# Splits of the left operands as single steps over fourteen products, and the first operands and blocks of the down phase loaded apart

## The chip, the cores and the metric

The kernel runs on one core of one Trainium2 chip. Its engines are TensorE (PE; its weight loads are listed apart as PEld), VectorE (DVE), ScalarE (ACT), GpSimd (POOL) and SyncE (SP, which here only issues DMAs). The metric is the device time of one execution in microseconds (us), the median of several runs; less is better. All times of single instructions come from one profiled execution.

## The reference, cut to what matters

One layer of an encoder for 1024 tokens of width 1024: a half-step feed-forward block, a mixer (two groups of attention heads), and a second half-step feed-forward block. The change lies in the two feed-forward blocks alone:

```python
def _swiglu(x, w_gate, w_up, w_down):
    return (jax.nn.silu(x @ w_gate) * (x @ w_up)) @ w_down
...
    f = _swiglu(_rmsnorm(x, ffn1_pre_g[l]), ffn1_w_gate[l], ffn1_w_up[l], ffn1_w_down[l])
    x = x + 0.5 * _rmsnorm(f, ffn1_post_g[l])
...
    f = _swiglu(_rmsnorm(x, ffn2_pre_g[l]), ffn2_w_gate[l], ffn2_w_up[l], ffn2_w_down[l])
    x = x + 0.5 * _rmsnorm(f, ffn2_post_g[l])
```

`w_gate` and `w_up` are 1024 x 2816, `w_down` is 2816 x 1024, all float32.

## The kernel before, in words

**Arithmetic.** Every large product is made of float32r matmuls on operands that are split in two: a high part (ACT rounds the number, `split`, L118) and a low part (the number less the high part, L119, on POOL or DVE). Three passes, high x high, high x low and low x high, make one product (`PASSES`). A feed-forward block is multiplied by a 2x2 block scheme with seven products in place of eight, so sums and differences of blocks are needed on both sides.

**Gate/up phase** (`gate_up`). The 2816 hidden columns are 22 blocks of 128, i = 0 to 21. Block 0 is done plainly. Each block from 1 to 21 is seven products P1, P6, P2, P7, P5, P4, P3, in this order (`ORDER`; the last block has `LAST`), and each product is 12 matmuls of 128x512 (`product`, L294). They share four PSUM banks: P1 and P2 lie in bank a, P6 in b, P7 and P4 in c, P5 and P3 in d (`BANK`), and the second product of a bank adds to what stands there. So three results must be read out before a later product may go on: P1's copy (ACT, L417) before P2; P7's addition (DVE, L422) before P4; P5's addition (DVE, L425) before P3. Each has one other product in between as cover. P2, P5, P4 and P3 end in `glu`: an ACT silu (L452) and a DVE multiplication (L453), which makes the hidden values `h` (DVE's L431 and L434 come ahead of those of P4 and P3). The left operands of later products (weights) are made five ahead (`feed`, `prepare`): ACT makes the high part `wgu`, POOL (for P5 and P3 DVE) the low one, and POOL also makes the differences of the weights (L218, L219 for P6, L228, L230 after P2) that the high parts of the next block wait for.

**Left operands of the down phase** (`keep`). Two blocks, 2j and 2j+1, make pair j (0 to 10). Their four `h` tiles give seven left operands S0 to S6: S0, S1 and S4 are `h` tiles, S5 = S5 + S4, S2 = S5 - S0 (in a new tile of the pool `dn`), S3 = S4 - S2 and S6 = S1 - S2 (L343). Each is split into a row of `y` and stored to DRAM as `hd` (L347), one queue on SP. `keep` puts seven steps into the list `late`, each of them the sum, the high part, the low part and the store of one operand. `run` takes one step off the list ahead of each product, so that in the text the steps of pair j stand at the seven products of the even block 2j+2, and the seven products of the next odd block have none. The steps of the last pair are all done at the end of block 21.

**Order.** The text gives each instruction a place. The order on each engine is fixed when the program is built, and an instruction may be drawn ahead of its place in the text when what it reads is there and its engine has nothing else to do. The tiles of a pool (`dn` has 10 for `h`) are handed out in the order of the text. On the chip each engine then runs its instructions strictly in that fixed order.

**Down phase** (`down`). 77 products of 12 matmuls (L370), k for the operand and j for the pair: first group j = 0 to 4 with k in the order 1, 0, 2, 3, 6, 4, 5, then j = 5 to 10. Each needs two tiles of the left operand from DRAM (`load_left`, L249) and a split right operand made from blocks of `w_down` (`load_block`, L240; `prepare_down`). The first two left operands (`AHEAD`) are loaded into `dn` after the fourth product of block 21, the next three after its last one and behind the steps of the last pair.

Of the kernel before, what the change touches and what calls it, by code (L numbers as in the profile page):

```python
# [10 lines left out]
F32 = mybir.dt.float32  # L11
# [8 lines left out]
S = 1024  # L20
# [16 lines left out]
def tile_macaron_block(ctx, tc, x, f1_pre, f1_post, f1_g, f1_u, f1_d, mix_pre, mix_post, w_qkv,  # L37
# [10 lines left out]
    def f32(ap):  # L48
        return ap.bitcast(F32)
# [71 lines left out]
    class Ffn:  # L121
# [14 lines left out]
        BLOCKS = ("b11", "b12", "b21", "b22")  # L136
        WBUFS = 5
        HBUFS = 10
        AHEAD = 2

        def __init__(self, wg, wu, wd, tag, far):
            self.wg, self.wu, self.wd, self.tag, self.far = wg[0], wu[0], wd[0], tag, far
# [96 lines left out]
            r = self.B[j, name] = self.dw[name].tile([128, 512], F32, name=name)  # L239
            SP.dma_start(r, self.wd[128 * (2 * j + c):128 * (2 * j + c) + 128, 512 * b:512 * b + 512])  # L240

        def load_left(self, n):

            for _ in range(n):
                if self.wanted:
                    key = self.wanted.pop(0)
                    self.A[key] = [self.dn.tile([128, 512], FR, name="h") for _ in range(2)]
                    for z, t in enumerate(self.A[key]):
                        SP.dma_start(f32(t), self.hd[key][:, 512 * z:512 * z + 512])  # L249

        def prepare_down(self, k, j):

            sub, add, tt = OP.subtract, OP.add, DVE.tensor_tensor
            n = len(self.GROUPS[0])
            after = [z for z in ((n,) if j == 0 else ()) + (j + n + 1,) if j < n and z < self.PAIRS]
            if k == 1 and j < n:
                for b in ("b22", "b12", "b11"):
                    self.load_block(j, b)
            b11, b12, b21, b22 = [self.B[j, name] for name in self.BLOCKS]
            self.split_w((j, k), (b11, b21, b11, b12, b12, b11, b22)[k], DVE)  # L260

            def diff(j):
                tt(self.B[j, "b12"], self.B[j, "b22"], self.B[j, "b12"], op=sub)

            if k == 1 and j < n:
                diff(j)
            elif k == 0:
                tt(b11, b12, b11, op=add)
            elif k == 3:
                tt(b12, b21, b11, op=sub)  # L270
            elif k == 4:
                tt(b11, b22, b11, op=sub)
            for z in after:
                for b in {3: ("b21",), 4: ("b12", "b22"), 5: ("b11",)}.get(k, ()):
                    self.load_block(z, b)
                if k == 5:
                    diff(z)
# [56 lines left out]
        def keep(self, j, y):  # L334

            a11, a21, a12, a22 = [self.H[2 * j + c][b] for c in range(2) for b in range(2)]
            S = {0: a11, 1: a12, 4: a22, 5: a21, 3: y[:, 7, 0:512], 6: y[:, 7, 512:1024]}

            def made(n, k, p=None, q=None, op=None):
                if op:  # L340
                    if k == 2:
                        S[k] = self.dn.tile([128, 512], F32, name="h")
                    DVE.tensor_tensor(S[k], S[p], S[q], op=op)  # L343
                st = y[:, n, :]
                hi, lo = [st[:, 512 * z:512 * z + 512].bitcast(FR) for z in range(2)]
                split(hi, lo, S[k], DVE)
                SP.dma_start(self.hd[k, j], st)  # L347

            for n, z in enumerate(((0,), (1,), (4,), (5, 5, 4, OP.add), (2, 5, 0, OP.subtract),
                                   (3, 4, 2, OP.subtract), (6, 1, 2, OP.subtract))):  # L350
                self.late.append(lambda n=n, z=z: made(n, *z))

        def down(self, k, js, y, ps, psd, row=None):
            g = js[0] in self.GROUPS[1]
# [48 lines left out]
        def gate_up(self, i, prod, ps, y, psd):  # L403
# [32 lines left out]
            if i == NF - 1 and n == 3:  # L436
                self.close_tx(3)
                self.raw.release()
                self.load_left(self.AHEAD)
                self.open_blocks(("b11", "b12"), self.far)  # L440
                self.open_blocks(("b22", "b21"), self.near)
                for j in self.GROUPS[0]:
                    self.load_block(j, "b21")
            if n == 6 and i % 2 == 1:
                self.keep(i // 2, y)
            if n == 6 and i == NF - 1:
                self.add_late(7)
                self.load_left(self.HBUFS // 2 - self.AHEAD)
                self.U = [U(name).rearrange("p t f -> p (t f)") for name in ("U2", "U2", "C21", "U3")]

        def glu(self, dst, c, s):
# [3 lines left out]
        def run(self, ps, y, psd, jobs, row):  # L455


            last = self.GROUPS[1][-2:]
            at = self.items.index(("D", 1, self.GROUPS[1][0]))
            for n, it in enumerate(self.items):  # L460
                if n == at:
                    self.add_late(len(self.late))
                    for name in ("b12", "b11"):
                        self.dw[name].release()
                self.feed()
                if not at - 18 <= n < at - 12:
                    self.add_late(1)
                if it[0] == "G":
                    self.gate_up(*it[1:], ps, y, psd)
                    self.used += 1  # L470
                elif it[1:] == (6, last[0]):
                    self.down(6, last, y, ps, psd, row)
                    break
                else:
                    self.down(it[1], it[2:], y, ps, psd)
                    self.used += 1
                    self.load_left(1)
                for job in jobs.get(n - at, ()):
                    job()
            for name in ("b21", "b22"):  # L480
# [726 lines left out]
```

## Time and profile before

| | us |
|---|---|
| median of 3 runs (2145.53 to 2147.35) | 2147.19 |
| profiled execution, own time | 2140.81 |
| its span in the trace | 2139.0 |
| PE busy | 1987.4 |
| DVE busy | 1438.1 |
| ACT busy | 1035.4 |
| POOL busy | 854.3 |

Both feed-forward blocks have the same form: the gate/up phase of the first runs from about 61 us to 524 us of the span, that of the second from about 1431 us to 1902 us, and a down phase follows each. A row of the waits names who waited for whom, and how long in total. A row of the timeline has the start, the length, the engine, the line, the tiles written and read, and in brackets how long the engine had been idle and what ended that. The clock granted to TensorE in the profiled execution was 0.989 of full speed in the mean.

### The profile page before, as it was taken

To read this page: it belongs to the slowest core of one execution; us is meant where nothing else is said; L and a number is where in the kernel's file an instruction comes from. 1 tells how busy PE (TensorE), PEld (TensorE's weight loads), DVE (VectorE), ACT (ScalarE), POOL (GpSimd) and SP (SyncE) were. 2 spreads that over 40 slices of the span, in tenths; PEclk is the share of its full clock that TensorE was granted. 3 is DMA by queue.
4 is the path that set the end of the run, shared out by engine and by line. 5 is a ranking of instruction groups with operands and counts; after the bars stand their busy time and mean duration, and the time that the engine had idled before them with its cause. 6 is when DMAs were issued, how large, how long until landed. Compare 5 with 4: busy or idle time off the path is not lost.

```text
span 2139.0 us, 30720 instructions
## 1 busy us (share of the span) xinstructions
PE 1987.4 (93%) x10704; PEld 1677.0 (78%) x10704; DVE 1438.1 (67%) x2431; ACT 1035.4 (48%) x1977; POOL 854.3 (40%) x768
## 2 busy tenths in 40 slices
PE   7899888998999999999999999999988899879997
PEld 6777667776788899998999998877766777658886
DVE  7765676657555757766998886466567665665566
ACT  5543443434222644546999997344343433433223
POOL 4556555563000002024777886225546555520000
PEclk9999999999899999999999999999999999989999
DMA  4343343435875853232041553213343333468757
GB/s 138 108 138 109 135 141 128 138 109 211 295 261 194 307 160 96 73 104 63 1 134 62 159 141 98 92 48 128 109 147 137 130 128 109 148 245 280 243 194 278
DMA packets 234618, 316.40 MB, mean 148 GB/s; under 512 B 24672, under 2 KB 150624, under 8 KB 234336
## 3 DMA queue, kind: packets, MB, share of 16 engines
q1 hardware_dynamic: 234464, 314.44, 44.0%
q8 instruction: 85, 1.39, 0.3%
q14 instruction: 69, 0.57, 0.1%
HBM read 206.38 MB, written 108.00 MB: 147 GB/s over the span
## 4 chain that ended last, share of the span: by engine, by line
PE 60%; DVE 15%; POOL 9%; ACT 7%; issue 5%; DMA 3%; SPq 0%; DVEq 0%; POOLq 0%; ACTq 0%
PE pd L370 9%; PE pq L612 9%; PE pa L294 6%; PE pt L937 5%; POOL wgu L119 4%; PE pz L1075 4%; PE pd L294 3%; PE pb L294 3%; ACT wgu L118 3%; PE pa L370 3%; PE pb L370 3%; PE po L961 3%; PE pc L370 3%; DVE y L119 3%; DVE y L343 3%
## 5 line engine op out<-in xcount | busy, mean ns | idle before, releaser
L119 POOL TENSOR_TENSOR wgu<-rawgu,wgu 128x512 fp32r<-128x512 f32 x216 | 304.9, 1420 | 449.9 <-ACT wgu L118 435.4
L118 ACT ACTIVATE wgu<-rawgu 128x512 fp32r<-128x512 f32 x302 | 186.4, 625 | 271.9 <-POOL rawgu L230 127.6
L294 PE MATMUL pa<-actT,wgu 128*128 128x512 f32 (+1 forms) x1080 | 269.1, 397 | 48.8 <-ACT U L417 47.9
L294 PEld LDWEIGHTS pa<-actT,wgu 128*128 128x128 f32 x1080 | 199.8, 190 | 103.2 <-ACT U L417 56.8
L370 PE MATMUL pd<-wgu,h 128*128 128x512 f32 x948 | 232.6, 391 | 0.0
L118 ACT ACTIVATE wgu<-b 128x512 fp32r<-128x512 f32 x154 | 96.7, 630 | 276.9 <-PE pd L370 265.4
L612 PE MATMUL pq<-wq,actT 128*128 128x256 f32 x1728 | 214.2, 281 | 0.7 <-DVE vst L623 0.7
L370 PEld LDWEIGHTS pd<-wgu,h 128*128 128x128 f32 x948 | 178.8, 189 | 37.8 <-DVE U L434 0.5
L612 PEld LDWEIGHTS pq<-wq,actT 128*128 128x128 f32 x1728 | 205.9, 188 | 1.0 <-DVE vst L623 0.9
L119 DVE TENSOR_TENSOR wgu<-b,wgu 128x512 fp32r<-128x512 f32 x154 | 105.8, 689 | 147.1 <-ACT wgu L118 146.9
L294 PE MATMUL pc<-actT,wgu 128*128 128x512 f32 x552 | 141.0, 405 | 39.7 <-DVE U L422 39.7
L294 PEld LDWEIGHTS pc<-actT,wgu 128*128 128x128 f32 x552 | 104.3, 192 | 71.9 <-ACT y L118 47.5
L73 POOL TENSOR_SCALAR gpost<-gpost 128x1024 f32<-128x1024 f32 x2 | 2.7, 1330 | 394.8 <-DMA gpost<-in_ffn_post_g_dram 394.8
L840 POOL TENSOR_SCALAR P<-P,il 128x1024 f32<-128x1024 f32 (+1 forms) x128 | 130.1, 1017 | 68.5 <-DVE il L839 62.2
L941 DVE TENSOR_TENSOR PT<-pt,PT 128x512 fp32r<-128x512 f32 (+1 forms) x256 | 146.1, 612 | 2.0 <-ACT PT L940 2.0
L294 PE MATMUL pd<-actT,wgu 128*128 128x512 f32 x552 | 137.4, 397 | 9.4 <-DVE U L425 9.4
L119 DVE TENSOR_TENSOR y<-h,y 128x512 fp32r<-128x512 f32 x110 | 111.2, 1012 | 44.6 <-ACT y L118 44.6
L294 PEld LDWEIGHTS pd<-actT,wgu 128*128 128x128 f32 x552 | 102.1, 188 | 40.3 <-issue 16.7
L940 ACT ACTIVATE PT<-pt 128x512 fp32r<-128x512 f32 (+1 forms) x256 | 125.1, 543 | 12.7 <-PE pt L937 8.6
L937 PE MATMUL pt<-identr,P 128*128 128x128 f32 x896 | 125.4, 275 | 3.1 <-ACT vst L775 2.4
L294 PE MATMUL pb<-tx,wgu 128*128 128x512 f32 x504 | 122.9, 392 | 0.0
L294 PE MATMUL pc<-tx,wgu 128*128 128x512 f32 x504 | 122.5, 392 | 0.0
(205 smaller groups left out, 4024.1 us busy)
## 6 DMA issues: line engine op xcount, KB each, us to landing
hd<-y SPq DMA_DIRECT2D x154, 512.0 KB, 2.7
h<-hd SPq DMA_DIRECT2D x308, 256.0 KB, 3.6
rawgu<-in_ffn_w_gate_dram SPq DMA_DIRECT2D x88, 256.0 KB, 3.1
rawgu<-in_ffn_w_up_dram SPq DMA_DIRECT2D x88, 256.0 KB, 3.5
b<-in_ffn_w_down_dram SPq DMA_DIRECT2D x88, 256.0 KB, 4.5
bkT<-kd SPq DMA_DIRECT2D x32, 320.0 KB, 7.1
rawq<-in_w_qkv_dram SPq DMA_DIRECT2D x16, 512.0 KB, 5.0
bV<-vd SPq DMA_DIRECT2D x8, 640.0 KB, 4.1
```

Source lines behind the costliest of these rows:

```text
L118: ACT.activation(hi, raw, AF.Copy)
L119: return eng.tensor_tensor(lo, raw, f32(hi), op=OP.subtract).ins
L294: PE.matmul(p[:, c0:c1, :], w[:, a, k, :], self.rhs(name, b, k)[:, c0:c1, :], start=(first and n == 0), stop=(n == 11), skip_group_check=True)
L343: DVE.tensor_tensor(S[k], S[p], S[q], op=op)
L370: PE.matmul(p, A[a][:, 128 * i:128 * i + 128], B[:, b, :], start=(first and start and j == js[0] and n == 0), stop=(end and j == js[-1] an ...
L612: PE.matmul(p, actT[:, a, k, T, :], WQ[j][:, b, k, :], start=(n == 0), stop=(n == 23))
L840: POOL.tensor_scalar(P[:, 0:w], P[:, 0:w], il, 1.0, op0=OP.mult, op1=OP.mult)
L937: PE.transpose(out=p[:, j, :], in_=col(P, b0 + j), identity=ident)
L940: ACT.activation(hv, p[:, 0:n, :], AF.Copy)
L941: DVE.tensor_tensor(lv, p[:, 0:n, :], f32(hv), op=OP.subtract)
L961: PE.matmul(o, V[:, k, :], pt[:, a, k, :], start=(n == 0), stop=(n == 15))
L1075: PE.matmul(p[:, 512 * dh:512 * dh + 512], actT[:, a, c, T, :], WO[c][:, b, 512 * dh:512 * dh + 512], start=(n == 0), stop=(n == 23))
```

## The change

`keep` now cuts the same work into fourteen steps, two of them empty. A step holds at most one high part (ACT) and the low part and store of the operand before, or a low part and the next sum. `run` takes one step after each product of the gate/up phase in place of one ahead of it, so in the text the steps of a pair stand over the fourteen products of two blocks. The three sums S2, S3 and S6 and the tile of S2 thereby come later in the text: S2 stands behind P4 of the even block, S3 and S6 at the products of the odd block after it. At the start of the down phase three left operands (not two) are loaded ahead, into a pool `ax` of their own, and five more (not three) behind the last steps; the blocks b11, b22 and b12 of a pair j < 5 are loaded, and their difference is made, when the product k = 0 is prepared and not at k = 1, which needs b21 alone.

```diff
-        AHEAD = 2
+        AHEAD = 3
...
-        def load_left(self, n):
+        def load_left(self, n, pool=None):
...
-                    self.A[key] = [self.dn.tile([128, 512], FR, name="h") for _ in range(2)]
+                    self.A[key] = [(pool or self.dn).tile([128, 512], FR, name="h") for _ in range(2)]
...
-            if k == 1 and j < n:
-                for b in ("b22", "b12", "b11"):
+            if k == 0 and j < n:
+                for b in ("b11", "b22", "b12"):
                     self.load_block(j, b)
-            b11, b12, b21, b22 = [self.B[j, name] for name in self.BLOCKS]
+            b11, b12, b21, b22 = [self.B.get((j, name)) for name in self.BLOCKS]
...
-            if k == 1 and j < n:
-                diff(j)
-            elif k == 0:
+            if k == 0:
+                if j < n:
+                    diff(j)
                 tt(b11, b12, b11, op=add)
...
-            def made(n, k, p=None, q=None, op=None):
-                if op:
-                    if k == 2:
-                        S[k] = self.dn.tile([128, 512], F32, name="h")
-                    DVE.tensor_tensor(S[k], S[p], S[q], op=op)
-                st = y[:, n, :]
-                hi, lo = [st[:, 512 * z:512 * z + 512].bitcast(FR) for z in range(2)]
-                split(hi, lo, S[k], DVE)
-                SP.dma_start(self.hd[k, j], st)
-
-            for n, z in enumerate(((0,), (1,), (4,), (5, 5, 4, OP.add), (2, 5, 0, OP.subtract),
-                                   (3, 4, 2, OP.subtract), (6, 1, 2, OP.subtract))):
-                self.late.append(lambda n=n, z=z: made(n, *z))
+            def half(n, z):
+                return y[:, n, 512 * z:512 * z + 512].bitcast(FR)
+
+            def total(k, p, q, op=OP.subtract):
+                if k == 2:
+                    S[k] = self.dn.tile([128, 512], F32, name="h")
+                DVE.tensor_tensor(S[k], S[p], S[q], op=op)
+
+            def high(n, k):
+                ACT.activation(half(n, HI), S[k], AF.Copy)
+
+            def low(n, k):
+                DVE.tensor_tensor(half(n, LO), S[k], f32(half(n, HI)), op=OP.subtract)
+                SP.dma_start(self.hd[k, j], y[:, n, :])
+
+            steps = [[], [], [(high, 0, 0)], [(low, 0, 0), (high, 1, 1)], [(low, 1, 1), (total, 5, 5, 4, OP.add)],
+                     [(high, 2, 4)], [(low, 2, 4), (total, 2, 5, 0)], [(high, 3, 5)], [(low, 3, 5), (total, 3, 4, 2)],
+                     [(high, 4, 2)], [(low, 4, 2), (total, 6, 1, 2)], [(high, 5, 3)], [(low, 5, 3), (high, 6, 6)],
+                     [(low, 6, 6)]]
+            for step in steps:
+                self.late.append(lambda step=step: [f(*z) for f, *z in step])
...
             if i == NF - 1 and n == 3:
                 self.close_tx(3)
                 self.raw.release()
-                self.load_left(self.AHEAD)
                 self.open_blocks(("b11", "b12"), self.far)
                 self.open_blocks(("b22", "b21"), self.near)
+                self.ax = open_pool("ax" + self.tag, bufs=2 * self.AHEAD, side=self.far)
+                self.load_left(self.AHEAD, self.ax)
...
-                self.add_late(7)
-                self.load_left(self.HBUFS // 2 - self.AHEAD)
+                self.add_late(len(self.late))
+                self.load_left(self.HBUFS // 2)
...
+            at0 = self.items.index(("D", 1, 0))
             for n, it in enumerate(self.items):
                 if n == at:
                     self.add_late(len(self.late))
+                    self.ax.release()
...
-                if not at - 18 <= n < at - 12:
+                if n > at0 and not at - 18 <= n < at - 12:
                     self.add_late(1)
                 if it[0] == "G":
                     self.gate_up(*it[1:], ps, y, psd)
                     self.used += 1
+                    self.add_late(1)
...
-                    self.load_left(1)
+                    if self.used - at0 > self.AHEAD:
+                        self.load_left(1)
```

## Rows read from the trace of the kernel before

**Rows 1.** Waits of PE: who waited for whom, total us, times, longest.

```profile
PE pa L294 <- ACT U L417: 47.9, 22, 2.3
PE pc L294 <- DVE U L422: 39.7, 20, 2.0
...
PE pa L370 <- DMA h<-hd: 19.1, 4, 6.0
```

**Rows 2.** Stretches of blocks 11, 12, 13: length, busy PE, PEld, DVE, ACT, POOL.

```profile
282.11:301.57 19.46, 19.46 (x86) 15.78 (x85) 8.84 (x13) 7.17 (x12) 10.83 (x9) 1.00 0.26 81
301.57:326.58 25.01, 20.17 (x85) 15.53 (x84) 19.96 (x21) 11.05 (x19) 14.24 (x11) 1.00 0.47 169
326.58:346.05 19.47, 19.47 (x86) 15.78 (x85) 8.80 (x13) 7.17 (x12) 10.82 (x9) 1.00 0.26 82
```

**Rows 3.** Timeline of ACT, blocks 11 to 13.

```profile
290.90 0.59 ACT L452 ACTIVATE h<-pa 64x512 f32<-64x512 f32 x1 [2.18 <-PE pa L294]
...
302.63 0.63 ACT L118 ACTIVATE wgu<-rawgu 128x512 fp32r<-128x512 f32 x1 [4.66 <-POOL rawgu L230]
...
308.64 0.63 ACT L118 ACTIVATE y<-h 128x512 fp32r<-128x512 f32 x1 [0.75 <-DVE h L453]
309.18 0.58 ACT L417 ACTIVATE U<-pa 128x512 f32<-128x512 f32 x1
...
312.92 0.59 ACT L452 ACTIVATE h<-pa 64x512 f32<-64x512 f32 x1 [1.60 <-PE pa L294]
...
325.74 0.63 ACT L118 ACTIVATE wgu<-rawgu 128x512 fp32r<-128x512 f32 x1 [1.22 <-POOL rawgu L230]
327.14 0.63 ACT L452 ACTIVATE h<-C 64x512 f32<-64x512 f32 x1 [0.77 <-DVE C L431]
328.52 0.63 ACT L118 ACTIVATE y<-h 128x512 fp32r<-128x512 f32 x1 [0.75 <-DVE h L453]
...
331.23 0.60 ACT L417 ACTIVATE U<-pa 128x512 f32<-128x512 f32 x1
...
335.38 0.59 ACT L452 ACTIVATE h<-pa 64x512 f32<-64x512 f32 x1 [2.18 <-PE pa L294]
```

**Rows 4.** Timeline of DVE, blocks 12 and 13.

```profile
308.64 0.69 DVE L343 TENSOR_TENSOR h<-h 128x512 f32<-128x512 f32 x1
...
310.83 1.37 DVE L119 TENSOR_TENSOR y<-h,y 128x512 fp32r<-128x512 f32 x1 [0.83 <-ACT y L118]
...
313.32 0.68 DVE L343 TENSOR_TENSOR h<-h 128x512 f32<-128x512 f32 x1
...
316.01 1.78 DVE L119 TENSOR_TENSOR y<-h,y 128x512 fp32r<-128x512 f32 x1
317.71 1.76 DVE L343 TENSOR_TENSOR y<-h 128x512 f32<-128x512 f32 x1
319.51 0.69 DVE L422 TENSOR_TENSOR U<-U,pc 128x512 f32<-128x512 f32 x1
...
329.80 0.68 DVE L434 TENSOR_TENSOR U<-U,pd 128x512 f32<-128x512 f32 x1
```

**Rows 5.** Timeline of POOL: one line in block 11 and in block 12.

```profile
294.84 1.29 POOL L219 TENSOR_TENSOR rawgu<-rawgu 128x512 f32<-128x512 f32 x1
...
317.32 1.61 POOL L219 TENSOR_TENSOR rawgu<-rawgu 128x512 f32<-128x512 f32 x1
```

**Rows 6.** Timeline of PE, start of the first down phase.

```profile
523.83 0.86 PE L370 MATMUL pa<-wgu,h 128*128 128x512 f32 x3
...
535.51 1.19 PE L370 MATMUL pa<-wgu,h 128*128 128x512 f32 x2 [6.00 <-DMA h<-hd]
...
542.15 0.80 PE L370 MATMUL pa<-wgu,h 128*128 128x512 f32 x1 [2.89 <-DMA h<-hd]
```

**Rows 7.** Timeline of DVE, end of block 21.

```profile
527.69 1.90 DVE L263 TENSOR_TENSOR b<-b,b 128x512 f32<-128x512 f32 x3
...
532.52 0.69 DVE L343 TENSOR_TENSOR h<-h 128x512 f32<-128x512 f32 x1
```

## What was predicted

> **What bounds the kernel now.** I read the waits of PE first, because PE is the busiest engine and every other engine matters only where PE stands still for it. In the gate/up phases PE waits for two things above all: the ACT copy of P1 (L417), 47.9 us, and the DVE addition of P7 (L422), 39.7 us; at the start of the two down phases it waits 19.1 us for left operands from DRAM [rows 1]. Then the stretches of single blocks, to see where. Odd blocks (11, 13) take 19.46 us, all of it PE: 7 products of 2.78 us. The even block 12, where the text has the operand steps, takes 25.01 us with PE busy for 20.17 [rows 2]. The pattern repeats, so a pair of blocks takes 44.48 us where PE alone needs 38.92. With ten pairs in each of two feed-forward blocks, 5.56 x 20 = 111 us is the most that the gate/up phases could give back.
>
> Third, the timelines of ACT and DVE through such a pair, to see what makes PE wait. I cut the pair at the silu of P2, since a chain starts there. In the **first half**, odd to even, the silu stands at 290.90 and 312.92: 22.02 us. In the **second half**, even to odd, at 312.92 and 335.38: 22.46 us [rows 3]. Both are longer than 19.46. From the silu of P2, ACT makes the high part of the next P1's weights, POOL its low part and differences L218 and L219, ACT and POOL the next two weights, POOL L228 and L230, and only then ACT the next high part: at 302.63 (11.73 us after the silu) and at 325.74 (12.82 us). The silus of P4 and P3 and the copy of P1 are queued on ACT behind that. The copy ends at 309.76 and 331.83, and 3.16 and 3.55 us later comes the next silu of P2 [rows 3]. The first half is thus 11.73 + 7.13 + 3.16, the second 12.82 + 6.09 + 3.55, where about 0.4 of the last term is slack (3.55 less 3.16). So in the first half the chain through ACT and POOL sets the time, and PE waits at P2. In the second half PE is late by itself, because P4 had to wait for L422, which stood on DVE behind operand instructions of 1.78 and 1.76 us [rows 4], and the copy comes just in time.
>
> **What the change moves.** The text spreads the steps, but the order on the engines isn't that of the text. The high part at 328.52 belongs to S0 of the pair 12/13: its place in the text is at P1 of block 14, after 346, and it runs as soon as P4's multiplication has made the tile [rows 3]. S4's high part likewise runs at 308.64, the moment it can, ahead of the copy of P1 at 309.18 that PE waits for [rows 3], though its place is two products behind it; S5's sum follows at 308.64 on DVE [rows 4]. A later place in the text doesn't hold such an instruction back. So S0, S1, S4 and S5 should stay where they are, and with them the first half: I cost it at 22.02, no change.
>
> S2 is the exception. Its inputs are there when S5's sum ends (309.33), and DVE idles for 0.83 us before 310.83, yet S2 runs at 313.32, right after the silu of P2 at 312.92 [rows 3, 4]. That silu is the first to write the `h` tile that is handed out ahead of S2's tile. After the change P5's tile is handed out first as well, and P5's multiplication is the first to write it. S2 then can't come before that, and S2's split, S3 and S6 with their splits hang on it. These are three sums and three low parts on DVE, and three high parts on ACT, which move by two products, from between P2 and P4 to between P5 and the next P1.
>
> What goes: L422 no longer stands behind them, so P4's wait (39.7 us in all) and the smaller one at P3 go. L219 shows 1.29 us with DVE idle and 1.61 with DVE's sums running [rows 5], so POOL's chain gets shorter ahead of P5. What is late next is the copy of P1 of the odd block, since now PE comes sooner and the six DVE instructions stand nearer to it. The second half afterwards:
> - Silu of P2 to the high part behind L230: 11.73 as in the first half, where no operand work runs beside it. DVE's sums now meet up to four POOL instructions (two low parts, L228, L230), 0.32 us each: 11.73 to 13.01. I take two, 12.37.
> - From there to the end of the copy: 6.09 now. It can lose the 0.77 us that ACT waits for L431 and the 1.28 from S0's high part (328.52) to L434 (329.80) [rows 3, 4], if S0 gets behind L434: 4.04. It can gain a sum of 1.76 [rows 4] and a high part of 0.63 with nothing lost: 8.48. I take 4.04 + 0.63 for S3's high part + 0.7 for one sum that meets no POOL instruction, 5.4, because P4's multiplication, which S0 waits for, gets later too.
> - P2 itself to its silu: 3.16 when PE waits for the copy.
>
> The sum is 20.93, against 22.46: 1.53 per pair, 31 us for 20 pairs. Bounds: 11.73 + 4.04 + 3.16 = 18.93 is under PE's 19.46, so at best 3.00 per pair, 60 us; 13.01 + 8.48 + 3.16 = 24.65 costs 2.19 per pair, 44 us. I lean from 31 to 28, since the last pair of each phase has block 21 with its own order.
>
> The stores go with the low parts on SP. I cost them at nothing: of PE's long waits none is for a load of weights [rows 1]. If a late store stood ahead of a weight load, the high part of the next P1 would wait, and that would be part of the 44 us.
>
> **Start of the down phase.** PE begins at 523.83, does two products, waits 6.00 us until 535.51 for the third left operand and 2.89 before 542.15 for its low tile [rows 6]; the second feed-forward block has the other 10.2 us of the 19.1 [rows 1]. Three operands loaded ahead give PE a product of 2.78 us more: 2 x 2.78 = 5.6 us is the least saving. The most is all 19.1. Further, the fourth operand takes `dn` tiles of the pair before the last, so it waits for no tile of the last pair, only for S2's tile to be handed out. S2 at 532.52 stood behind the differences of the blocks, three in 1.90 us at 527.69 and one more [rows 7], which now get a place behind the steps: S2 about 2.5 us sooner. So 2 x (2.78 + 2.5) = 10.6 for certain work, and about half of the low tiles' waits: I take 15. Two more tile loads on SP ahead of the blocks are hidden under the last three products of block 21; without that cover they would lengthen the same wait. The blocks b11, b22 and b12 can be fetched as soon as their pools open, wherever the text has them; were b11 late, ACT's split for k = 0 would hold up only splits behind it, five products ahead of PE.
>
> Sum: 28 + 15 = 43 us. The profiled execution took 2140.8, 6.4 under the median of the runs; taken off the median, 2147.2 - 43 = **2104 us** (the profiled execution would be near 2098).
>
> **Rivals.** Measurements of this kernel tell 0.2%, 4.3 us, from no change.
> - *Both halves at PE's pace.* The steps really spread and no wait is left: 111 + 15 = 126 us, 2021. For it: DVE is busy for 28.8 us and ACT for 18.2 of a pair's 44.5 [rows 2]. Against it: the first half has S4's high part ahead of the copy, and nothing holds it back.
> - *The order stays.* If S2 was held by something else than its tile, DVE's order stays as it is and only the down phase gains: 2147 - 15 = 2132. For it: in the text of before, S2 also stands behind others. Against it: the idle 0.83 us of DVE.
> - *Slower: the copy of the odd block is held up.* The six DVE instructions meet POOL between P5 and the next P1 and stand ahead of P4's multiplication and L434. At the upper bound this costs 44 us and leaves 44 - 15 = 29: 2176. It decides from 0.75 us per pair on (15 / 20): a second half above 23.2 us, which is the copy's end more than 20.0 us after the silu of P2. For it: operand instructions take up to 1.78 us in place of 0.69 where POOL runs beside them [rows 4]. Against it: P5 to P1 leaves DVE about 11 us.
> - The Trainium skill (SBUF — State Buffer, section "Who interferes with whom") has a rule that speaks for this rival: a VectorE instruction with both inputs in SBUF and a GpSimd one that reads SBUF take turns on one port pair, and the loser stands still for the whole of the other. By that an operand instruction could take up to 0.69 + 1.29 = 1.98 us, an estimate; the trace agrees so far as its longest of these rows is 1.78, and L422 and L434, which read PSUM, stay at 0.69.
>
> **How the numbers follow.** Forecast as above, 0.62, by itself from 2068 (60 + 19) to 2138; order stays 0.13; both at PE's pace 0.08; slower 0.12; the two terms cancel within 0.2%, 0.05. Faster is 0.62 + 0.13 + 0.08 = 0.83. The range 2066 to 2148 holds the forecast, the kept order and the cancelling, 0.80, and leaves out the two far cases.
>
> **What would show it.** Right: even blocks lose the wait before P4 (L422's row near nothing), the wait of P2 for L417 stays in even blocks and appears in odd ones, S2 runs right after P5's multiplication, a pair takes about 43 us; the first down wait falls below 2 us. Wrong: L417's wait gone in even blocks (then far faster), S2 still beside the silu of P2 (then only the down phase moves), or a pair above 44.5 us.

## The result, and the profile after

The kernel after takes **2117.24 us** (median of 4 runs, 2112.03 to 2119.59), the kernel before on the same chip 2146.36 (4 runs). The ratio is 0.986, 95% interval 0.984 to 0.988: 29 us or 1.4% faster. The forecast was 2104 with a range of 2066 to 2148. In the profiled executions the span goes from 2139.0 to 2117.1, 21.9 less. PE's busy time rises by 12.2 us to 1999.6, though no matmul is added, and the mean granted clock falls from 0.989 to 0.981.

First the waits of PE after the change (who waited for whom, total us, times, longest). L425 is the copy of P1, L378 a matmul of the down phase, L118 ACT's rounding to a high part.

```profile
PE pa L294 <- ACT U L425: 61.7, 40, 2.6
PE pa L378 <- DMA h<-hd: 14.6, 2, 7.3
...
PE pa L378 <- ACT wgu L118: 5.2, 2, 2.9
```

The row of P7's addition, 39.7 us in [rows 1], is gone. The copy's wait is there 40 times in place of 22: in both blocks of a pair. The wait for left operands has lost 4.5 us, but one for ACT's split has come up.

The windows of block 11, of the even block 12, and then of P2 alone in block 12 and in block 4 (length, busy PE, PEld, DVE, ACT, POOL, granted clock, DMA share, GB/s):

```profile
271.20:291.67 20.47, 19.72 (x86) 15.69 (x85) 13.52 (x18) 8.74 (x15) 12.86 (x11) 1.00 0.45 154
291.67:315.23 23.56, 21.25 (x86) 16.84 (x85) 13.28 (x16) 9.36 (x16) 12.05 (x9) 0.93 0.34 112
...
299.93:304.40 4.47, 4.47 (x13) 3.52 (x14) 2.75 (x4) 1.50 (x3) 1.29 (x1) 0.62 0.87 312
...
127.12:129.80 2.68, 2.68 (x12) 2.19 (x13) 1.85 (x3) 1.51 (x3) 1.31 (x1) 1.00 0.95 331
```

A pair took 19.46 + 25.01 in [rows 2]; it is 20.47 + 23.56 now. The operand work is spread over both: DVE is busy for 13.5 and 13.3 us, where it was 8.8 and 20.0. The third row is P2 of block 12: 4.47 us at a granted clock of 0.62, a mean of stretches at 2.4 and at 1.2 GHz. The last row is the same product in block 4: 2.68 us at 1.00. From block 4 to block 18, even blocks without such a fall take 22.04 us, those with one 23.56.

The timeline of ACT, through block 12 to the silu of P2 in block 13 (L461 silu, L348 an operand's high part):

```profile
281.00 0.59 ACT L461 ACTIVATE h<-pa 64x512 f32<-64x512 f32 x1 [2.12 <-PE pa L294]
...
292.75 0.63 ACT L118 ACTIVATE wgu<-rawgu 128x512 fp32r<-128x512 f32 x1 [4.66 <-POOL rawgu L230]
...
298.76 0.63 ACT L348 ACTIVATE y<-h 128x512 fp32r<-128x512 f32 x1 [0.75 <-DVE h L462]
299.30 0.58 ACT L425 ACTIVATE U<-pa 128x512 f32<-128x512 f32 x1
...
304.58 0.59 ACT L461 ACTIVATE h<-pa 64x512 f32<-64x512 f32 x1 [3.14 <-PE pa L294]
...
317.00 0.63 ACT L118 ACTIVATE wgu<-rawgu 128x512 fp32r<-128x512 f32 x1 [2.23 <-POOL rawgu L230]
...
321.29 0.60 ACT L425 ACTIVATE U<-pa 128x512 f32<-128x512 f32 x1
...
325.05 0.59 ACT L461 ACTIVATE h<-pa 64x512 f32<-64x512 f32 x1 [2.12 <-PE pa L294]
```

S4's high part still runs at the moment it can, just ahead of the copy (298.76, 299.30), as at 308.64 and 309.18 in [rows 3]. The second half, 304.58 to 325.05, is 20.47 us.

The timeline of DVE at the same place (L345 the sums, L351 the low parts, L439 the addition ahead of P4's silu):

```profile
311.70 0.71 DVE L462 TENSOR_TENSOR h<-C,U 64x512 f32<-64x512 f32 x1 [0.96 <-ACT C L461]
312.42 1.69 DVE L345 TENSOR_TENSOR h<-h 128x512 f32<-128x512 f32 x1
314.14 1.67 DVE L345 TENSOR_TENSOR y<-h 128x512 f32<-128x512 f32 x1
315.73 0.68 DVE L439 TENSOR_TENSOR C<-U,pc 128x512 f32<-128x512 f32 x1
...
322.50 1.83 DVE L351 TENSOR_TENSOR y<-y 128x512 fp32r<-128x512 f32 x1
```

S2 now runs right behind P5's multiplication (311.70, 312.42). In [rows 4] it stood at 313.32, after P2.

The start of the first down phase, on PE and on SP's queue:

```profile
511.96 0.56 PE L378 MATMUL pa<-wgu,h 128*128 128x512 f32 x1 [2.27 <-ACT wgu L118]
...
529.93 1.62 PE L378 MATMUL pa<-wgu,h 128*128 128x512 f32 x3 [7.35 <-DMA h<-hd]
```

```profile
492.24 7.45 SPq L352 DMA_DIRECT2D hd<-y  x4
499.77 1.83 SPq L240 DMA_DIRECT2D b<-in_ffn_w_down_dram  x2
501.70 2.85 SPq L249 DMA_DIRECT2D h<-hd  x6
504.82 7.46 SPq L240 DMA_DIRECT2D b<-in_ffn_w_down_dram  x10
...
519.84 5.13 SPq L352 DMA_DIRECT2D hd<-y  x5
525.02 9.81 SPq L249 DMA_DIRECT2D h<-hd  x12
```

Three operands are ahead, so three products run before the long wait and not two; but the wait is 7.35 us where [rows 6] had 6.00 and then 2.89, and one of 2.27 us stands in front of the first matmul (2.95 in the second phase).

### The profile page after: what moved, and what is told of

Read it like the earlier page. It is cut to its first block, busy times and chain, and to the rows that moved or that the text cites. A ratio compares the mean times of both kernels' runs of the same rounds, so it can differ in the third digit from the quotient of the medians.

```text
span 2117.1 us, 30680 instructions
## 1 busy us (share of the span) xinstructions
PE 1999.6 (94%) x10704; PEld 1692.5 (80%) x10704; DVE 1399.4 (66%) x2431; ACT 1032.7 (49%) x1977; POOL 849.5 (40%) x768
## 5 line engine op out<-in xcount | busy, mean ns | idle before, releaser
L119 POOL TENSOR_TENSOR wgu<-rawgu,wgu 128x512 fp32r<-128x512 f32 x216 | 309.4, 1441 | 435.8 <-ACT wgu L118 428.7
L294 PE MATMUL pa<-actT,wgu 128*128 128x512 f32 (+1 forms) x1080 | 289.5, 419 | 61.7 <-ACT U L425 61.7
L118 ACT ACTIVATE wgu<-rawgu 128x512 fp32r<-128x512 f32 x302 | 182.6, 625 | 317.3 <-POOL rawgu L219 155.8
L294 PEld LDWEIGHTS pa<-actT,wgu 128*128 128x128 f32 x1080 | 211.2, 202 | 126.1 <-ACT U L425 78.2
L378 PE MATMUL pd<-wgu,h 128*128 128x512 f32 x948 | 231.1, 390 | 0.0
L118 ACT ACTIVATE wgu<-b 128x512 fp32r<-128x512 f32 x154 | 96.2, 630 | 257.9 <-PE pd L378 227.0
L378 PEld LDWEIGHTS pd<-wgu,h 128*128 128x128 f32 x948 | 177.9, 188 | 37.4 <-DVE U L442 0.5
L294 PE MATMUL pc<-actT,wgu 128*128 128x512 f32 x552 | 136.5, 396 | 0.0
L953 ACT ACTIVATE PT<-pt 128x512 fp32r<-128x512 f32 (+1 forms) x256 | 125.0, 543 | 13.5 <-PE pt L950 11.0
L351 DVE TENSOR_TENSOR y<-h,y 128x512 fp32r<-128x512 f32 x110 | 101.7, 925 | 30.6 <-ACT y L348 30.6
```

What stands on the lines that cost most here:

```text
L118: ACT.activation(hi, raw, AF.Copy)
L119: return eng.tensor_tensor(lo, raw, f32(hi), op=OP.subtract).ins
L294: PE.matmul(p[:, c0:c1, :], w[:, a, k, :], self.rhs(name, b, k)[:, c0:c1, :], start=(first and n == 0), stop=(n == 11), skip_group_check=True)
L351: DVE.tensor_tensor(half(n, LO), S[k], f32(half(n, HI)), op=OP.subtract)
L378: PE.matmul(p, A[a][:, 128 * i:128 * i + 128], B[:, b, :], start=(first and start and j == js[0] and n == 0), stop=(end and j == js[-1] an ...
L953: ACT.activation(hv, p[:, 0:n, :], AF.Copy)
```

## Experiments

Steps are those of `keep`. A "fall" is a product at a granted clock below 1.00 behind a wait of PE. In the expectations, e4 is the experiment with the high parts behind the copy, e9 the one with both edits, e8 the order of the loads, and e10 the sums behind P3's multiplication.

**The steps alone.** The kernel after with the start of the down phase as before:

```diff
-        AHEAD = 3
+        AHEAD = 2
...
-            if k == 0 and j < n:
-                for b in ("b11", "b22", "b12"):
+            if k == 1 and j < n:
+                for b in ("b22", "b12", "b11"):
...
+                self.load_left(self.AHEAD)
...
-                self.ax = open_pool("ax" + self.tag, bufs=2 * self.AHEAD, side=self.far)
-                self.load_left(self.AHEAD, self.ax)
...
-                self.load_left(self.HBUFS // 2)
+                self.load_left(self.HBUFS // 2 - self.AHEAD)
...
```

> The fourteen steps of the change, with the start of the down phase as it was before. Theory: the whole gain of 29 us is made in the gate/up phases, because S2, S3 and S6 move behind P5, and the new start of the down phase trades its waits for others and nets nothing. Then this run is near the changed kernel, 2114 to 2124 us. Rival, the prediction's second term: the down phase gives 15 us, and this run is 2128 to 2136.

Measured 2127.13 us, ratio 0.990 (0.989 to 0.992): between the two. The gate phases lose 20.2 us of their span. But from the end of the last gate product to the start of the sixteenth product of the down phase, the two phases together take 117.8 us where the kernel before takes 110.0, although nothing of the down phase was changed. PE waits 2.06 and 3.27 us in front of the first product, where it had no wait, and 11.36 and 11.38 us for the third operand in place of 6.00 and 5.96. So the spread steps themselves cost 7.8 us there. The timeline of PE, first phase:

```profile
533.97 1.62 PE L378 MATMUL pa<-wgu,h 128*128 128x512 f32 x3 [11.36 <-DMA h<-hd]
```

**The down phase alone.** The kernel before with the new start of the down phase, and `keep` with its seven steps.

> The steps as before, the start of the down phase as in the change. Theory (the down phase nets nothing): 2142 to 2150 us, with a wait for b21 or for the fourth left operand where the third was waited for. Rival (it gives 10 to 19 us): 2128 to 2137.

Measured 2136.64, ratio 0.994 (0.993 to 0.996): 11 us less than the kernel before beside it, as its rival said. PE has no wait in front of the first product, and the first fifteen products take 50.15 and 51.81 us in place of 54.62 and 55.66: 8.3 us less.

**Seven steps, those from S2 on one product later.** The kernel before with one empty step:

```diff
             for n, z in enumerate(((0,), (1,), (4,), (5, 5, 4, OP.add), (2, 5, 0, OP.subtract),
                                    (3, 4, 2, OP.subtract), (6, 1, 2, OP.subtract))):
+                if n == 4:
+                    self.late += [lambda: None]
                 self.late.append(lambda n=n, z=z: made(n, *z))
...
-                self.add_late(7)
+                self.add_late(len(self.late))
```

> The kernel before with one edit: an empty step ahead of S2's, so that S2's sum and its tile come behind P5's tile in the text; the seven undivided steps still stand at eight neighbouring products and ahead of them. Theory (the first write of S2's tile can't come ahead of that of P5's tile; nothing else of the spreading counts): S2 runs right behind P5's multiplication, PE's wait for L422 goes, and most of the gate gain is there, about 0.6 to 1.5 us per pair: 2116 to 2134 us. S6's high part stands ahead of the copy of P1 here, so it may fall short of the changed kernel. Rival (steps cut apart and put behind the products make the gain): 2142 to 2150 us.

Measured 2170.01, ratio 1.011 (1.009 to 1.012): slower, neither the theory's time nor the rival's. S2 did move (280.60, right behind P5's multiplication at 279.87), and the row of L422 went, as in the kernel after. But here a high part waits for its sum in front of the copy (timeline of ACT, L419 is the copy), so PE waits longer in the second half. The wait is 2.1 us in the mean in all 40 blocks:

```profile
290.41 0.63 ACT L118 ACTIVATE y<-y 128x512 fp32r<-128x512 f32 x1 [0.52 <-DVE y L343]
290.94 0.58 ACT L419 ACTIVATE U<-pa 128x512 f32<-128x512 f32 x1
```

```profile
PE pa L294 <- ACT U L419: 85.5, 40, 2.3
```

A block without a fall takes about 21.8 us, a pair 43.7, less than the 44.48 before. But 26 blocks, 13 in each phase, have a fall and take 23.4 to 23.6. The windows of one with a fall and of one without:

```profile
283.44:306.89 23.45, 21.27 (x86) 16.84 (x84) 13.33 (x18) 8.84 (x15) 12.72 (x10) 0.93 0.39 134
261.60:283.44 21.84, 19.72 (x86) 15.71 (x85) 13.33 (x16) 9.36 (x16) 11.89 (x9) 1.00 0.36 122
```

26 x 1.6 = 42 us. Without them 2128 would be left, an estimate, inside what was expected. So by this count the same move of S2 can win or lose, and what decides is whether PE's waits are followed by falls.

**A filler for the wait.** The kernel after with eight matmuls ahead of P2 of the even blocks 4 to 20, into a bank that nothing reads; they add work and change no result.

```diff
+            if prod == "P2" and 2 < i < NF - 1 and i % 2 == 0:
+                junk = psd.tile([128, 4, 128], F32, name="pd")
+                for k in range(8):
+                    PE.matmul(junk, self.W[i, "P6"][:, HI, k % 4, :], self.rhs("T2", HI, k % 4),
+                              start=(k == 0), stop=(k == 7), skip_group_check=True)
```

> The changed kernel with 8 matmuls of 128x512, whose result nothing reads, between P6 and P2 of the even blocks from 4 on: 1.85 us of PE work in its 2.3 us wait for the copy. Theory (P2 takes 4.2 us in place of 2.7 in 14 blocks because the granted clock fell after the wait): the clock stays up, P2 takes 2.7, and 14 x 1.5 us are saved: 2093 to 2102 us. Rival (P2 is slow for what runs beside it, the stores and loads above all): P2 stays slow, 2112 to 2122 us.

Measured 2097.75, ratio 0.977 (0.975 to 0.979): 19.5 us faster than the kernel after with more work on PE. P2 comes no sooner (the copy releases it as before), but it runs at 1.00. The rows are the timeline of PE and the window of that P2:

```profile
296.69 3.07 PE L294 MATMUL pa<-actT,wgu 128*128 128x512 f32 x12 [0.50 <-ACT U L430]
```

```profile
296.68:299.36 2.68, 2.67 (x12) 2.17 (x12) 1.85 (x3) 1.51 (x3) 1.29 (x1) 1.00 0.98 339
```

Of the 18 even blocks with the filler 17 take 21.99 to 22.05 us (block 20 of the first phase takes 22.31), and no block has a fall. That the falls cost some 20 us is shown by this.

**S2 in a tile of its own.** The kernel after with

```diff
-                    S[k] = self.dn.tile([128, 512], F32, name="h")
+                    S[k] = self.dn.tile([128, 512], F32, name="s2", bufs=1)
```

> The changed kernel with S2 in a tile of its own in place of one of the ten for h; its place in the text stays behind P4. Theory (S2 waits only because the first writes of the shared tiles go in the order of the text): S2 runs right behind S5's sum, S3 and S6 follow it in the first products of the even block, and the second half of a pair loses the operand sums beside POOL: 19.5 to 20.2 us in place of 20.45; 2097 to 2112 us. Rival (the place in the text holds it): S2 stays behind P5's multiplication, 2112 to 2121 us.

Measured 2128.26, ratio 0.991 (0.989 to 0.993): the order came as expected, the time did not. S2's sum no longer waits for P5's multiplication and runs 0.6 us behind S5's; it is the shared pool that sets its place. The timeline of DVE (L345 the sums, first S5's, then S2's into its tile `s`):

```profile
307.97 0.69 DVE L345 TENSOR_TENSOR h<-h 128x512 f32<-128x512 f32 x1
...
309.25 0.69 DVE L345 TENSOR_TENSOR s<-h 128x512 f32<-128x512 f32 x1
```

But the operand work crowds ahead of P7's addition again, and both waits of PE stand side by side (L425 the copy, L430 P7's addition):

```profile
PE pa L294 <- ACT U L425: 72.3, 39, 2.4
PE pc L294 <- DVE U L430: 18.2, 12, 2.8
```

**High parts behind the copy.** The kernel after, where a high part may not stand ahead of the last copy that was written down before it:

```diff
             def high(n, k):
-                ACT.activation(half(n, HI), S[k], AF.Copy)
+                with tc.issue_after(self.copied):
+                    ACT.activation(half(n, HI), S[k], AF.Copy)
...
-                ACT.activation(s["u2"], p, AF.Copy)
+                self.copied = ACT.activation(s["u2"], p, AF.Copy).ins
```

> The changed kernel with the high parts of the left operands queued on ACT behind the copy of P1 of the next block, in place of as soon as they can run. Theory (in the first half of a pair the high parts of S1 and S4, and the low part of S1 that L434 stands behind, hold the copy back by about 2.5 us): PE no longer waits at P2 of even blocks, and P2 no longer runs slowly there; first half 19.5 to 20.5 us in place of 22.0 to 23.6, so 45 to 75 us less: 2042 to 2072 us. Rival (the chain through POOL alone sets the 22 us): less than 1 us per pair, 2097 us or more.

Measured 2058.53, ratio 0.959 (0.957 to 0.960). The even block of a pair takes 19.75 us, the odd one 20.95, 40.7 where the kernel after takes 42.5 even without a fall; the mean clock is 0.993 and P2 shows no fall. So in the first half it was the high parts in front of the copy that cost 2.3 us, and not the chain through POOL alone.

**Both of these.** The high parts held, and S2 in a tile of its own.

> e4 (high parts queued behind the copy of P1) and S2 in a tile of its own together. Theory: e4's second half, 20.95 us, loses the operand sums between P5 and the next P1 and comes to 19.5 to 20.2: 15 to 29 us under e4's 2058.5, 2030 to 2044. Rival (DVE's six sums and low parts now delay the first additions of the even block): 2052 us or more.

Measured 2111.10, ratio 0.983 (0.981 to 0.986): the rival. Odd blocks are at PE's pace (19.46), but now P7's addition (L431) stands behind operand instructions on DVE, the last two of them 3.44 us; even blocks take 22.85, and 24.4 with a fall. PE waits 59.4 us in 20 times for it. The timeline of DVE:

```profile
305.26 3.44 DVE L352 TENSOR_TENSOR y<-h,y 128x512 fp32r<-128x512 f32 x2
...
309.46 0.69 DVE L431 TENSOR_TENSOR U<-U,pc 128x512 f32<-128x512 f32 x1
```

**Order of the loads.** The kernel after, with each block of b21 loaded right behind its operand tile and the fourth and fifth operands ahead of the last steps:

```diff
-                self.load_left(self.AHEAD, self.ax)
                 for j in self.GROUPS[0]:
+                    if j < self.AHEAD:
+                        self.load_left(1, self.ax)
                     self.load_block(j, "b21")
...
+                self.load_left(2)
                 self.add_late(len(self.late))
-                self.load_left(self.HBUFS // 2)
+                self.load_left(self.HBUFS // 2 - 2)
```

> The changed kernel with two moves at the end of block 21: each block b21 is loaded right behind the left operand of its product in place of behind all three, and the fourth and fifth left operands are loaded ahead of the last pair's steps. Theory (the first product of the down phase waits about 3 us for b21, whose load stands behind six operand loads, and the fourth for operands whose loads stand behind the stores of the last steps): both waits shrink, 6 to 16 us in the two phases: 2101 to 2112 us. Rival (the transfers themselves are the limit, 0.75 MB for each product of 2.78 us): the waits move to a later product, 2112 us or more.

Measured 2111.62, ratio 0.984 (0.982 to 0.986): 5.6 us less than the kernel after in the medians. That is the edge of the theory's range. The first fifteen products take 49.2 and 49.3 us in place of 52.0 and 52.1, 2.8 less each, and the wait of 7.35 us is one of 0.88. The wait in front of the first product stays (2.04 and 1.98 us). What releases PE there is P2's multiplication (L464), whose silu (L463) stands on ACT behind a split of b21, and that split still waits for its load:

```profile
512.05 0.63 ACT L118 ACTIVATE wgu<-b 128x512 fp32r<-128x512 f32 x1 [6.87 <-DMA b<-in_ffn_w_down_dram]
512.71 0.59 ACT L463 ACTIVATE h<-pa 64x512 f32<-64x512 f32 x1
...
514.18 0.96 PE L378 MATMUL pa<-wgu,h 128*128 128x512 f32 x3 [2.04 <-DVE h L464]
```

**Sums behind P3's multiplication**, with the high parts held; then the same with the order of loads above. In the list of steps, not shown here, the three sums now stand together, behind the high part of S5.

```diff
             def total(k, p, q, op=OP.subtract):
...
+                if k == 5:
+                    DVE.tensor_tensor(S[k], S[p], S[q], op=op)
+                else:
+                    with tc.issue_after(self.glued):
+                        DVE.tensor_tensor(S[k], S[p], S[q], op=op)
...
-            DVE.tensor_tensor(dst, s[64:128], c[64:128], op=OP.mult)
+            self.glued = DVE.tensor_tensor(dst, s[64:128], c[64:128], op=OP.mult).ins
```

> e4 with the sums S2, S3 and S6 queued on DVE behind P3's multiplication of the even block, in place of between P5 and P4. Theory (in e4's second half of 20.95 us these sums run beside POOL's last four instructions and hold up the chain to the copy): second half 19.5 to 19.9 us, as e9 showed 19.46 with the sums gone from there, and no wait for L422's addition, since the even block's first products keep the order of e4; 20 pairs x 1.0 to 1.4: 2030 to 2040 us. Rival (the low parts of S2, S3 and S6 now come later and crowd the odd block's first additions): 2050 us or more.

> e10 with the order of the loads of e8. Theory: the order of the loads is worth about what it was on the changed kernel, 5 to 6 us: 2025 to 2035 us, 5 to 6 below e10. Rival (with the high parts queued early the stores no longer hold up the loads, so nothing is left to win): within 2 us of e10.

Measured 2071.24 (0.965, 0.962 to 0.967) and 2070.60 (0.965, 0.963 to 0.967): 13 us slower than with the sums where they were, and the loads change nothing. The sums no longer run beside POOL's L228 and L230, which take 1.28 and 1.29 us in place of 1.63 and 1.62, and the odd block falls from 20.95 to 20.30 us. But the even one goes from 19.75 to 21.03. ACT's timeline in block 11 (L353 is the high part of an operand) shows where it went:

```profile
268.61 0.63 ACT L353 ACTIVATE y<-h 128x512 fp32r<-128x512 f32 x1 [0.32 <-DVE h L349]
270.31 1.23 ACT L353 ACTIVATE y<-y 128x512 fp32r<-128x512 f32 x2 [1.08 <-DVE y L349]
271.45 0.62 ACT L118 ACTIVATE wgu<-rawgu 128x512 fp32r<-128x512 f32 x1
272.09 0.59 ACT L466 ACTIVATE h<-pa 64x512 f32<-64x512 f32 x1
```

The high parts wait 0.32 and 1.08 us on ACT for the sums, which come later now, and behind them stand a high part of weights and the silu of P2, from which the next chain through POOL starts. Counted from silu to silu, as in the prediction, the second half is 21.45 us (250.64 to 272.09) where it is 20.95 without the edit: 0.5 us a pair, 10 of the 13 us.

**The copy ahead of P3's silu.** What was left with the high parts held shows in ACT's timeline of that kernel:

```profile
250.51 0.59 ACT L462 ACTIVATE h<-pa 64x512 f32<-64x512 f32 x1
...
267.05 0.63 ACT L462 ACTIVATE C<-U 64x512 f32<-64x512 f32 x1 [1.41 <-DVE U L443]
267.70 0.60 ACT L426 ACTIVATE U<-pa 128x512 f32<-128x512 f32 x1
...
271.46 0.59 ACT L462 ACTIVATE h<-pa 64x512 f32<-64x512 f32 x1 [0.56 <-PE pa L294]
```

The rows at 250.51 and 271.46 are P2's silus of blocks 10 and 11, 20.95 us apart. The copy (L426) stands behind the silu of the product P3 of the block before (267.05), which waits 1.41 us for DVE. The edit on top of it (`held` starts empty, and block 21 keeps its old order; those lines are left out):

```diff
-                s["u2"], s["c21"] = U("U2"), U("C21")
+                s["u2"] = U("U2")
                 self.copied = ACT.activation(s["u2"], p, AF.Copy).ins
+                if self.held:
+                    with tc.issue_after(self.copied):
+                        self.held.pop()()
+                s["c21"] = U("C21")
...
-                self.glu(s["h1"][0:64], s["u2"], s["c21"])
+                self.held = [lambda h=s["h1"], u=s["u2"], c=s["c21"]: self.glu(h[0:64], u, c)]
```

> What still holds TensorE in the version with the high parts held is, in both blocks of a pair, the copy of P1, which stands on ScalarE behind the silu of P3's product of the block before, and that silu waits for VectorE's addition to U2 (it started 0.09 us after that addition's end; the copy followed it at once). Here P3's silu and multiplication are issued behind the next block's copy. Theory (this silu is the last link): the copy comes 2.06 us sooner in the second half (265.64 in place of 267.70), which is more than TensorE's wait there (1.62 us over the 2.77 of a product) and in the first half (0.43 us); both blocks of a pair go to 19.45 to 19.6 us, the gate phases lose 35 to 42 us and the time is 2016 to 2026 us. Rival (the loop is another: GpSimd's two sums for the raw weights, 1.62 and 1.63 us, and ScalarE's high part behind them, still stand ahead of the copy, and GpSimd itself waits for products): the loop gets shorter by the silu alone (0.65 us a block) and blocks stay above 19.9 us: 2035 to 2050 us.

> The copy ahead of P3's silu, and beside it the loads at the start of the down phase in the order of the experiment on load order (each block of b21 right behind its operand tile, the fourth and fifth operands' loads ahead of the last steps). Theory (the loads are worth what they were worth by themselves, 5.6 us in the medians against the kernel after): 4 to 8 us less than the version with the copy first, beside which it runs. Rival (as with the sums held, where the same loads changed nothing: gaps went from 1.2 to 0.2 us and the gate phases took the same back): within 2 us of it.

Measured 2048.06 (0.954, 0.952 to 0.955) and 2048.87 (0.954, 0.952 to 0.956). The copy's row falls from 24.8 us to 3.8, and three of four blocks take 19.40 to 19.8 us. Most of the theory's blocks came, its time did not; the time lies in the rival's range, but for another reason. In every second even block P7's addition (L435) is late again, up to 2.0 us, behind two low parts (L352) that take 3.48 us (the wait of PE, then DVE's timeline in block 8). The loads are worth nothing here, as its rival said.

```profile
PE pc L294 <- DVE U L435: 17.4, 10, 2.0
```

```profile
209.04 3.48 DVE L352 TENSOR_TENSOR y<-h,y 128x512 fp32r<-128x512 f32 x2
...
213.27 0.69 DVE L435 TENSOR_TENSOR U<-U,pc 128x512 f32<-128x512 f32 x1
```

2048 us is the fastest version found, 4.65% under the kernel before and 3.3% under the kernel after. A version that also holds these low parts behind L435 was not tried.

## Why the prediction came out as it did

The direction and the mechanism were right, the size was not: 43 us were forecast, 29 came in the medians and 21.9 in the two spans. By spans, the gate/up phases gave 21.1 us, and the start of the down phases 0.6. That the time came out as near as it did is in part luck: a second half that gave 9 us more than its 31 makes up for a part of what two terms had wrong, the lower clock in the first half and the start of the down phase.

- **The order: right.** S0, S1, S4 and S5 stayed, S2 moved behind P5's multiplication (312.42). That the hold is the shared pool is shown by the tile of its own; that it isn't the number of steps, by the single empty step, which moved S2 alike.
- **The second half: right, a little better than forecast.** By its terms: silu of P2 to the high part behind L230, 12.42 us (304.58 to 317.00; forecast 12.37); to the end of the copy at 321.89, 4.89 (forecast 5.4); copy to silu 3.16 (forecast 3.16). That is 20.47 in place of 20.93, and 1.99 us less than before: 20 pairs give 40 us.
- **The first half: the step that failed.** It was costed at "22.02, no change". Its order is unchanged, 11.75 and 7.13 us, and where the clock holds, an even block takes 22.04. But 14 times (6 and 8) P2 ran partly at the lower clock, 1.53 us more each, 21 us. 40 less 21 is 19, near the 21.1 of the spans. The filler gave back 19.5. The forecast had no term for the clock: its rows were those of blocks 11 to 13, which show 1.00 throughout. But the same trace has two falls, at P4 of block 2 in each phase (0.62 and 0.61), which took 4.6 us there (row in the last section) and 3.0 in the other even blocks behind the same wait of 1.98 us. The prediction also had the chain through ACT and POOL set the first half; that is not all of it, since the even block takes 19.75 us with that chain in place and the high parts held.
- **The down phase: mis-sized, 15 forecast, 0.6 measured.** From the end of the last gate product to the start of the sixteenth down product, the two phases together take 110.0 us in the kernel before, 101.6 with the new start alone, 117.8 with the steps alone and 109.3 with both. So the new start is worth 8.3 us with the old steps and 8.5 with the new ones: the two terms do add up. What is missing is a cost of the steps at this border, 7.8 us, and the forecast had put their stores at nothing. With the steps spread, block 21 has stores of the pair before; on SP's queue they stand ahead of b21 (492.24, 499.77), the last of them until its low part is made (499.34), and ACT's split of b21 waits for it until 511.28. With the high parts held, only two such stores are left there (0.92 us), and PE's wait in front of the first product is 0.51 and 0.57 us. The six operand tiles of the new start stand ahead of most of b21 as well (501.70, 504.82). Of the 15 itself, "certain work" of 10.6 took S2 to come 2.5 us sooner; it came 7.8 us behind the first product in place of 8.7. The fourth operand's load stood behind the last stores on SP instead (519.84, 525.02), and PE waited 7.35 us for it, so the sign "below 2 us" did not come.
- **The rivals.** *Copy held up* was put at 0.12. It did not happen here; but the empty step, which asks for the same move of S2, made a version of it, 22 us slower than before. The price came less from the wait than from the clock behind it. *Both halves at PE's pace* was refused because S4's high part stands ahead of the copy, and that was right: holding the high parts back alone is worth 58.7 us over the kernel after, of which some 21 are the falls that go with it.

By the Trainium skill (SBUF — State Buffer, "Who interferes with whom"), a DVE instruction with both inputs in SBUF and a POOL one that reads SBUF take turns; the estimate from that was up to 1.98 us for an operand instruction. The longest row here is 1.83 (322.50), the two sums beside POOL are 1.69 and 1.67, and L439, which reads PSUM, stayed at 0.68 in between: the trace agrees.

## What to carry to other kernels

A text that spreads work does not by itself spread it on the engines: look for what actually holds an instruction (here the first write to a shared pool), and for what of it stands ahead of the one instruction that the bottleneck waits for. Holding small work back behind that copy gave twice what the change did, and each wait removed brought up the next one in line, P3's silu, then P7's addition. A change of one phase can cost at the start of the next when both issue on one queue: list what stands on the queue at the border.

## What the runs showed of the hardware

A wait of PE of about 2.3 us was followed by a lower granted clock in some blocks and not in others with the same wait, in one execution of the kernel after: 1.00 in P2 of block 4 after 2.33 us, 0.62 in that of block 12 after 2.31 us, and 0.62 in that of block 10 after 2.33 us again. The timeline of PE for blocks 4 and 12, whose windows are shown above:

```profile
127.12 3.07 PE L294 MATMUL pa<-actT,wgu 128*128 128x512 f32 x12 [2.33 <-ACT U L425]
...
299.93 4.61 PE L294 MATMUL pa<-actT,wgu 128*128 128x512 f32 x12 [2.31 <-ACT U L425]
```

With the wait cut to 0.50 us by work that nobody needed, no even block showed it. What separates the two cases in one execution stays open. The kernel before has it as well: its profiled execution shows the two falls at P4 of block 2, at a mean clock of 0.989. The first of them, at 0.62:

```profile
97.19 4.58 PE L294 MATMUL pc<-actT,wgu 128*128 128x512 f32 x12 [1.98 <-DVE U L422]
```

Beside the experiments it took 2140.7 us at a mean clock of 0.988 and 2150 to 2152 us at 0.982 to 0.985, with most executions in between. That more falls in those executions are why the medians differ by more than the spans is likely, but not shown: where their clock fell is not on record.
